# Projections that take turns in four PSUM banks, recurrence sums in the transposes' banks, and a difference issued behind a weight split

## The chip, the core and the metric

The kernel runs on one core of one Trainium2 chip. The metric is the device time of one execution in microseconds (us); the time before is a median of three executions. The profile comes from one further execution of the same program.

## What is computed

The kernel is a trunk of two layers over x with 1024 positions and 1024 channels, all in float32. Cut to what matters here, a layer is:

```
def hybrid_layer(x, ...):
    h = rms_norm(x, norm1_g)
    proj = h @ w_in                       # 4 mLSTM heads of 128, 8 attention heads of 64
    qk = silu(conv(concat([mq, mk])))     # centred depthwise conv, width 5
    h_fwd = mlstm_chunkwise(q, k, v, gi[0], gf[0])
    h_bwd = flip(mlstm_chunkwise(flip(q), flip(k), flip(v), ...))
    y_m = head_norm(h_fwd + h_bwd) * sigmoid(mo)
    y_a = dilated_attention(aq, ak, av)
    x = x + concat([y_m, y_a]) @ w_out
    u = relu(rms_norm(x, norm2_g) @ w_up)
    return x + (u * u) @ w_down
# inside mlstm_chunkwise, over the chunks of a direction:
    C_new = decay * C + einsum("bhs,bhsk,bhsv->bhkv", w, k_c, v_c)
    h = (s @ v + inter * (q @ C_prev)) / max(abs(den), exp(-m_t))
```

## The kernel before

Each float32 product of the projections and of the feed-forward is computed from parts. A weight tile of 128x512 is loaded, ScalarE casts it to the rounded part `wh` (line 80), GpSimd subtracts that from the weight to give the rest `wl` (line 82), and TensorE makes three matmuls for each slab of 128 channels: `wh` with the activations' high part (line 90), `wh` with their low part (line 91), and `wl` with the high part (line 92). In the output projection and the feed-forward the same three stand on line 835. A split's two instructions are given a high priority.

A projection of the mLSTM (`proj`, line 176) fills two banks of PSUM, one for each half of the 1024 positions. It loads the weights in two tiles of four slabs; for each tile it runs 12 matmuls into the bank of the first half and then 12 into that of the second. The banks come from a pool tagged `pj` with three buffers. VectorE empties a bank by multiplying with the norm's factors into SBUF (`evac_r`, line 174); such a tile is called z for q and k, so for the output gate and zv for the values.

For every head the order is: values (taken one head ahead), q, k, so (the output gate), then the values of the next head, and then the head's recurrence. After k's projection its conv (line 311) and SiLU (line 327) follow, and TensorE transposes k (line 361) and multiplies k with q (line 367) into tiles `pt` of the tag s, which has two buffers; ScalarE copies the transposes to `kn` (line 362) and VectorE multiplies the products into E (line 369). E also takes a transfer from the gates' table (E<-gd, line 344), a subtraction (line 345) and an exponential (line 347).

The recurrence runs over 8 chunks in two directions, one step of each direction in turn (14 steps that update the state). In a step TensorE adds two products into pn (line 383 with E, line 385 with the previous state C), and forms the new sum pk (line 394) in a bank of the tag t, which has one buffer; VectorE makes the new C out of it (line 399). The head before is closed (`m_tail`) around the start of the next recurrence; its multiplications and transposes stand on lines 414 to 431.

A scheduler decides the order of the instructions on each engine, from dependencies, the pools' buffers and priorities. The order in which the program is written and the priorities set it; `issue_after` holds instructions back until a given one has been placed.

The output projection and the feed-forward use a scheme with seven products of sums and differences of quarter matrices (`seven`, line 843; `products`, line 822, splits a weight tile and multiplies it). The first call in a layer (early) begins while the attention's last results are written: VectorE makes differences of y into T (lines 874, 793, 799), each of which is cast by ScalarE (line 783) and has its rest taken by VectorE (line 784), as operands b.

Of the kernel before, what the change touches and what calls it, by code (L numbers as in the profile page):

```python
# [12 lines left out]
F32 = mybir.dt.float32  # L13
# [6 lines left out]
P = 128  # L20
# [3 lines left out]
HALF = 512  # L24
# [8 lines left out]
NC = S // P  # L33
# [6 lines left out]
def bc(ap, shape):  # L40
    return ap.to_broadcast(shape)


class Trunk:
# [31 lines left out]
    def wsplit(self, raw):  # L76
        nc = self.nc
        with self.tc.high_priority(400):
            wh = self.wp.tile([P, 4, P], F32R, name="wh", tag="wh", bufs=3)
            nc.scalar.copy(wh, raw)  # L80
            wl = self.wp.tile([P, 4, P], F32R, name="wl", tag="wl", bufs=3)
            nc.gpsimd.tensor_tensor(out=wl, in0=raw, in1=wh.bitcast(F32), op=ALU.subtract)  # L82
        return wh, wl
# [7 lines left out]
        nc.tensor.matmul(ps, wh[:, j, :], xl[:, sl], start=False, stop=False)  # L91
        nc.tensor.matmul(ps, wl[:, j, :], xh[:, sl], start=False, stop=stop)  # L92

    def pj2(self):
        return [self.pj.tile([P, HALF], F32, name="pj", tag="pj", bufs=3) for _ in range(2)]


    def sumsq(self, acc, x, t, first, eng=None):
# [75 lines left out]
            self.nc.vector.tensor_tensor(out=out, in0=ps, in1=r[:, t * HALF:(t + 1) * HALF], op=ALU.mult)  # L174

    def proj(self, L, n, hs):
        ps = self.pj2()
        for i in range(2):
            w = self.wload(self.a["w_in"][L, n, :, 4 * i:4 * i + 4])
            for t in range(2):  # L180
                for j in range(4):
                    k = 4 * i + j
                    self.mm3(ps[t], w, j, hs[k], t, k == 0, k == KD - 1)
        return ps
# [4 lines left out]
    def gates(self, L, hs, acc, pl, order):  # L189

        nc = self.nc
        ps = [self.mx.tile([P, HALF], F32, name="ps", tag="s", bufs=2) for _ in range(2)]
# [4 lines left out]
                self.mm3(ps[t], ws[k // 4], k % 4, hs[k], t, k == order[0], k == order[-1])  # L197
        self.ws0 = None
        ws = [self.wload(self.a["w_in"][L, 4, :, 4 * i:4 * i + 4]) for i in range(2)]
        self.ahead = self.pj2()  # L200
        for t in range(2):
            for k in range(KD):
                if (t, k) == (1, (1, 0)[L]):
# [47 lines left out]
        for i in range(2):  # L251
            nc.vector.tensor_scalar(out=at[:, NC * i:NC * i + NC], in0=chunk, scalar1=v[:, i:i + 1], scalar2=None,
                                    op0=ALU.mult)
        pa = self.mx.tile([P, 2 * NC], F32, name="pa", tag="t", bufs=1)
        nc.tensor.matmul(pa, sel, at, start=True, stop=True)
        nc.vector.tensor_copy(st, pa)
        ML, BL = st[:, 0:NC], st[:, NC:2 * NC]
# [18 lines left out]
        pt = self.mx.tile([P, 3, NC, 16], F32, name="pt", tag="s", bufs=2)  # L276
# [6 lines left out]
    def m_values(self, L, h, hs, r, mp):  # L283
# [8 lines left out]
        return zv, v1  # L292

    def m_proj(self, L, h, hs, r, mp, gates, values):

        nc = self.nc
# [38 lines left out]
    def m_head(self, L, h, prj, nat, mp, pend):  # L335
        nc = self.nc
        q, k, so, v1 = prj
        G = lambda nm, shape: mp.tile(shape, F32, name=nm, tag="G", bufs=7)
        E, qi, dec = [], [], []
        for d in range(2):  # L340
            row = d * MH + h
            e = G("E", [P, NC, P])
            nc.sync.dma_start(e, bc(self.a["cm"][:, d:d + 1], [P, NC, P]))
            nc.gpsimd.dma_start(e, bc(self.gd[L][row, 0].unsqueeze(0), [P, NC, P]), accum_op=ALU.add)
            nc.vector.tensor_tensor(out=e, in0=nat[:, 0, :, row:row + 1].to_broadcast([P, NC, P]), in1=e,
                                    op=ALU.subtract)
            nc.scalar.activation(e, e, AF.Exp)
            E.append(e)
            x = G("qi", [P, S])
            nc.sync.dma_start(x.rearrange("p (c t) -> p c t", t=P), bc(self.gd[L][row, 1].unsqueeze(0), [P, NC, P]))  # L350
            dc = mp.tile([P, NC], F32, name="dec", tag="dec", bufs=4)
            nc.vector.tensor_copy(dc, x[:, (P - 1 if d == 0 else 0)::P])
            qi.append(x)
            dec.append(dc)
        for d in range(2):
            nc.vector.scalar_tensor_tensor(out=qi[d], in0=q, scalar=KSCALE, in1=qi[d], op0=ALU.mult, op1=ALU.mult)
        kn = G("kn", [P, NC, P])
        for g in range(2):
            pt = self.mx.tile([P, 4, P], F32, name="pt", tag="s", bufs=2)
            for c in range(4):  # L360
                nc.tensor.transpose(pt[:, c], k[:, (4 * g + c) * P:(4 * g + c + 1) * P], self.ident)
            nc.scalar.copy(kn[:, 4 * g:4 * g + 4], pt)
        for g in range(2):
            pt = self.mx.tile([P, 4, P], F32, name="pt", tag="s", bufs=2)
            for c in range(4):
                sl = slice((4 * g + c) * P, (4 * g + c + 1) * P)
                nc.tensor.matmul(pt[:, c], k[:, sl], q[:, sl], start=True, stop=True)
            for d in range(2):
                nc.vector.scalar_tensor_tensor(out=E[d][:, 4 * g:4 * g + 4], in0=pt, scalar=KSCALE,
                                               in1=E[d][:, 4 * g:4 * g + 4], op0=ALU.mult, op1=ALU.mult)  # L370
        if pend is not None:
            self.m_tail(*pend)
        H = [G("H", [P, NC, P + 2])[:, :, 0:P + 1] for d in range(2)]
        C = [None, None]
        pn = [None, None]
        for i in range(NC):
            for d in range(2):
                row = d * MH + h
                c = i if d == 0 else NC - 1 - i
                if i % 3 == 0:  # L380
                    pn[d] = self.mx.tile([P, 3, P + 1], F32, name="pn", tag="o", bufs=2)
                ps = pn[d][:, i % 3]
                nc.tensor.matmul(ps, E[d][:, c], v1[:, c], start=True, stop=i == 0)
                if i > 0:
                    nc.tensor.matmul(ps, qi[d][:, c * P:(c + 1) * P], C[d], start=False, stop=True)
                if i % 3 == 2 or i == NC - 1:
                    n = i % 3 + 1
                    dst = H[d][:, c - n + 1:c + 1] if d == 0 else H[d][:, c:c + n][:, ::-1]
                    nc.scalar.copy(dst, pn[d][:, :n])
                if i < NC - 1:  # L390
                    wv = mp.tile([P, P + 1], F32, name="wv", tag="wv", bufs=3)
                    nc.scalar.activation(wv, v1[:, c], AF.Copy, scale=nat[:, 1, c, row:row + 1])
                    pk = self.mx.tile([P, P + 1], F32, name="pk", tag="t", bufs=1)
                    nc.tensor.matmul(pk, kn[:, c], wv, start=True, stop=True)
                    Cn = mp.tile([P, P + 1], F32, name="C", tag=f"C{d}", bufs=2)
                    if i == 0:
                        nc.vector.tensor_copy(Cn, pk)
                    else:
                        nc.vector.scalar_tensor_tensor(out=Cn, in0=C[d], scalar=dec[d][:, c:c + 1],
                                                       in1=pk, op0=ALU.mult, op1=ALU.add)  # L400
                    C[d] = Cn
        return H
# [419 lines left out]
    def products(self, ws, parts, chain=False, ps=None, then=None):  # L822

        nc = self.nc
        new = ps is None
        res = []
        for q, w in enumerate(ws):
            out = self.bank(chain) if new else ps[q]
            wh, wl = self.wsplit(w)
            if then:  # L830
                then(q)
            for k in range(4):
                hi, lo = [x[:, k % 2] for x in parts[k // 2]]
                for i, (a, b) in enumerate(((wh, hi), (wh, lo), (wl, hi))):
                    nc.tensor.matmul(out, a[:, k, :], b, start=new and k + i == 0, stop=k + i == 5,  # L835
                                     skip_group_check=not new)
            res.append(out)
        return res
# [4 lines left out]
    def seven(self, src, B, op, take, nxt, early=False, end=None):  # L843
# [5 lines left out]
        T, T3 = [[self.up.tile([P, 2, HALF], F32, name="T", tag=tag, bufs=2) for _ in range(2)] for tag in ("T", "T3")]  # L849
# [12 lines left out]
        else:  # L862
# [4 lines left out]
            op = self.operand(B21)  # L867
# [3 lines left out]
        ps = self.products(w1, op)  # L871
# [3 lines left out]
        if not early:  # L875
            op = self.operand(T)
        take(2, ps)
        if not early:
            P5 = self.products(w2, op, then=addto(w2, 0, 0))
        op = self.negsum(T, B22)  # L880
        if not early:
            take(5, P5)
        chain = self.products(w2, op, True, chain, then=addto(w2, 0, 1))
        op = self.diff(T3, B22, B12)
        take(6, chain)
        chain = self.products(w0, op, True, chain)
        op = self.negsum(T, B21)
        take(7, chain)
        chain = self.products(w1, op, True, chain)
        op = self.operand(B22)  # L890
# [3 lines left out]
        ps = self.products(w2, op, ps=P5)  # L894
        op = nxt()
# [194 lines left out]
    def run(self):  # L1090
        tc, nc, a = self.tc, self.nc, self.a
        nc.scalar.preload_act_table_set("natural_log_exp_and_others")
        with tc.tile_pool(name="cst", bufs=1) as cp, tc.tile_pool(name="wp", bufs=1) as self.wp, \
                tc.tile_pool(name="hl", bufs=1) as self.hlp, tc.tile_pool(name="yx", bufs=1) as yxp, \
                tc.tile_pool(name="nrm", bufs=1) as self.nrm, tc.tile_pool(name="gnat", bufs=1) as self.gnat, \
                tc.tile_pool(name="pj", bufs=1, space=PSUM) as self.pj:
            self.L, self.pools = 0, ((yxp, "yx"), (self.hlp, "hl"))
            def const(nm, shape, eng=nc.sync):
                t = cp.tile(shape, F32, name=nm, tag=nm)
                eng.dma_start(t, a[nm])  # L1100
                return t
# [98 lines left out]
```

## Time and profile before

| | us |
|---|---|
| median of 3 executions | 2606.19 (2604.83 to 2611.5) |
| the profiled execution | 2613.41 |
| its span | 2611.6 |
| TensorE busy | 2456.4 |
| VectorE busy | 1906.1 |
| GpSimd busy | 1344.7 |
| ScalarE busy | 1244.6 |

The span is what the trace covers, from the first to the last instruction. Engines overlap, so busy times do not add up to it. A matmul of 128x512 is recorded with 0.39 us, but the matmuls overlap: one starts 0.23 us after the other at the full clock.

### The profile page before, as it was taken

Reading aid. Unit: us, or ns where it says so; the run is one execution under the profiler, and the core shown is the slowest. Engines: PE = TensorE matmul, PEld = TensorE weight load, DVE = VectorE, ACT = ScalarE, POOL = GpSimd, SP = SyncE. Lnnn points to the kernel's source line nnn. Section 1 sums busy time; section 2 is a strip of 40 time slices with the busy share of each in tenths; the row PEclk is TensorE's granted clock in tenths of the full one; section 3 lists DMA queues with packets and bytes.
Section 4 is the critical chain, followed back from the end, with each engine's and each line's share of the span. In section 5 each row is a group of like instructions: output and inputs, shape, how many; then the busy total and the mean of one; then the engine's idle time right before and its main releaser. Section 6 shows DMA issues by size and latency. Waiting matters only on the chain. (4 is left out here: it accounts for less than half of the span.)

```text
span 2611.6 us, 35935 instructions
## 1 busy us (share of the span) xinstructions
PE 2456.4 (94%) x13470; PEld 1952.3 (75%) x13470; DVE 1906.1 (73%) x2388; ACT 1244.6 (48%) x2068; POOL 1344.7 (51%) x1111
## 2 busy tenths in 40 slices
PE   7999989998999999999998999999899999999997
PEld 5778766666778888787776777666577787887876
DVE  6566776686886786968766666667768967679687
ACT  5444354454644545444543444445455445454554
POOL 4222332235676667767642223233276766667765
PEclk9999999998999999999999999999999999999998
DMA  4422100154555555555333221002455555545552
GB/s 144 119 81 81 43 25 22 40 140 105 102 108 115 105 108 104 111 106 115 96 112 98 81 81 39 21 24 80 109 117 98 108 108 114 106 108 104 110 102 80
DMA packets 136287, 239.65 MB, mean 92 GB/s; under 512 B 15008, under 2 KB 34480, under 8 KB 136112
## 3 DMA queue, kind: packets, MB, share of 16 engines
q0 software_dynamic: 49216, 101.45, 23.2%
q1 hardware_dynamic: 86896, 135.89, 17.0%
q8 instruction: 107, 1.75, 0.3%
q14 instruction: 68, 0.56, 0.1%
HBM read 228.50 MB, written 8.65 MB: 91 GB/s over the span
## 5 line engine op out<-in xcount | busy, mean ns | idle before, releaser
L82 POOL TENSOR_TENSOR wl<-w,wh 128x512 fp32r<-128x512 f32 x484 | 786.4, 1645 | 286.5 <-ACT wh L80 285.5
L835 PE MATMUL ph<-b,wh 128*128 128x512 f32 x2240 | 691.4, 390 | 0.2 <-ACT wh L80 0.2
L80 ACT CAST wh<-w 128x512 fp32r<-128x512 f32 x484 | 298.4, 618 | 415.2 <-PE ph L835 112.0
L835 PEld LDWEIGHTS ph<-b,wh 128*128 128x128 f32 x2240 | 421.1, 188 | 88.0 <-ACT wh L80 0.9
L835 PE MATMUL ph<-b,wl 128*128 128x512 f32 x1120 | 439.6, 393 | 9.7 <-POOL wl L82 9.2
L82 POOL TENSOR_TENSOR wl<-wr,wh 128x512 fp32r<-128x512 f32 x132 | 193.4, 1468 | 446.1 <-ACT wh L80 415.9
L835 PE MATMUL pj<-b,wh 128*128 128x512 f32 x1224 | 382.1, 394 | 22.9 <-ACT wh L80 14.9
L90 PE MATMUL pj<-hh,wh 128*128 128x512 f32 x896 | 369.2, 412 | 22.9 <-DVE z L174 21.8
L91 PE MATMUL pj<-hl,wh 128*128 128x512 f32 x896 | 357.4, 399 | 0.0
L92 PE MATMUL pj<-hh,wl 128*128 128x512 f32 x896 | 356.5, 398 | 0.7 <-POOL wl L82 0.7
L784 DVE TENSOR_TENSOR b<-T,b 128x1024 fp32r<-128x1024 f32 x144 | 249.0, 1733 | 120.4 <-ACT b L783 116.7
L835 PEld LDWEIGHTS pj<-b,wh 128*128 128x128 f32 x1224 | 231.9, 190 | 74.7 <-ACT wh L80 15.8
L835 PE MATMUL pj<-b,wl 128*128 128x512 f32 x612 | 241.2, 394 | 18.6 <-POOL wl L82 18.6
L835 PEld LDWEIGHTS ph<-b,wl 128*128 128x128 f32 x1120 | 210.6, 188 | 63.8 <-POOL wl L82 20.4
L90 PEld LDWEIGHTS pj<-hh,wh 128*128 128x128 f32 x896 | 171.1, 191 | 73.4 <-DVE z L174 24.4
L92 PEld LDWEIGHTS pj<-hh,wl 128*128 128x128 f32 x896 | 170.5, 190 | 36.5 <-POOL wl L82 1.6
L91 PEld LDWEIGHTS pj<-hl,wh 128*128 128x128 f32 x896 | 171.3, 191 | 30.8 <-issue 0.5
L783 ACT CAST b<-T 128x1024 fp32r<-128x1024 f32 x144 | 151.3, 1051 | 56.4 <-DVE T L799 20.5
L811 POOL DMA_DIRECT2D w<-w_down x128 | 117.3, 948 | 71.9 <-DMA w<-w_down 32.2
L617 ACT ACTIVATE sm<-sm,nm 128x512 f32<-128x512 f32 x128 | 91.6, 717 | 127.7 <-DVE nm L615 127.7
L835 PEld LDWEIGHTS pj<-b,wl 128*128 128x128 f32 x612 | 116.2, 190 | 47.1 <-POOL wl L82 22.8
L811 POOL DMA_DIRECT2D w<-w_up x128 | 115.0, 927 | 65.5 <-DMA w<-w_up 28.3
(256 smaller groups left out, 4159.9 us busy)
## 6 DMA issues: line engine op xcount, KB each, us to landing
w<-w_up SPq DMA_DIRECT2D x128, 256.0 KB, 2.7
w<-w_up POOLq DMA_DIRECT2D x128, 256.0 KB, 4.2
w<-w_down SPq DMA_DIRECT2D x128, 256.0 KB, 2.7
w<-w_down POOLq DMA_DIRECT2D x128, 256.0 KB, 4.3
wr<-w_in SPq DMA_DIRECT2D x116, 256.0 KB, 2.7
E<-cm SPq DMA_DIRECT2D x16, 512.0 KB, 5.8
qi<-gd SPq DMA_DIRECT2D x16, 512.0 KB, 7.0
E<-gd POOLq DMA_DIRECT2D x16, 512.0 KB, 7.2
```

The source lines that it names most:

```text
L80: nc.scalar.copy(wh, raw)
L82: nc.gpsimd.tensor_tensor(out=wl, in0=raw, in1=wh.bitcast(F32), op=ALU.subtract)
L90: nc.tensor.matmul(ps, wh[:, j, :], xh[:, sl], start=start, stop=False)
L91: nc.tensor.matmul(ps, wh[:, j, :], xl[:, sl], start=False, stop=False)
L92: nc.tensor.matmul(ps, wl[:, j, :], xh[:, sl], start=False, stop=stop)
L617: nc.scalar.activation(sm, sm, AF.Exp, scale=-1.0, bias=nm, accum_out=l)
L783: nc.scalar.copy(hi, src)
L784: nc.vector.tensor_tensor(out=lo, in0=src, in1=hi.bitcast(F32), op=ALU.subtract)
L811: self.nc.gpsimd.dma_start(w, src, accum_op=ALU.add)
L835: nc.tensor.matmul(out, a[:, k, :], b, start=new and k + i == 0, stop=k + i == 5, skip_group_check=not new)
```

## The change

Four edits are made. Every second projection of the mLSTM takes the bank of a new tile `pm` for its first half, with the tag t (one buffer), so four banks are used in turn: values pj and pj, q pm and pj, k pj and pj, so pm and pj. The sums `pk` and the gates' `pa` leave the tag t and take the tag s with its two buffers, which the transposes use. The copy of the transposed k to `kn` gets the high priority that weight splits have. In the early call of `seven`, the difference for the third product (`negsum`) is held back until the split of the third weight tile of the first product has been placed.

```diff
 def wsplit(self, raw):
-            nc.scalar.copy(wh, raw)
+            self.split = nc.scalar.copy(wh, raw).ins
...
-    def pj2(self):
-        return [self.pj.tile([P, HALF], F32, name="pj", tag="pj", bufs=3) for _ in range(2)]
+    def pj2(self, four=False):
+
+        res = []
+        for _ in range(2):
+            self.turn = (self.turn + 1) % 4
+            if four and self.turn == 3:
+                res.append(self.mx.tile([P, HALF], F32, name="pm", tag="t", bufs=1))
+            else:
+                res.append(self.pj.tile([P, HALF], F32, name="pj", tag="pj", bufs=3))
+        return res
...
     def proj(self, L, n, hs):
-        ps = self.pj2()
+        ps = self.pj2(True)
...
-        self.ahead = self.pj2()
+        self.ahead = self.pj2(True)
...
-        pa = self.mx.tile([P, 2 * NC], F32, name="pa", tag="t", bufs=1)
+        pa = self.mx.tile([P, 2 * NC], F32, name="pa", tag="s", bufs=2)
...
-            nc.scalar.copy(kn[:, 4 * g:4 * g + 4], pt)
+            with self.tc.high_priority(400):
+                nc.scalar.copy(kn[:, 4 * g:4 * g + 4], pt)
...
-                    pk = self.mx.tile([P, P + 1], F32, name="pk", tag="t", bufs=1)
+                    pk = self.mx.tile([P, P + 1], F32, name="pk", tag="s", bufs=2)
...
             wh, wl = self.wsplit(w)
+            if q == 2:
+                self.third = self.split
...
-        op = self.negsum(T, B22)
+        with self.tc.issue_after(self.third) if early else nullcontext():
+            op = self.negsum(T, B22)
```

What this does to the order of the instructions is shown at three places. Lines of the changed kernel stand 8 to 13 lower. The number of matmuls is the same.

On TensorE, this is the middle of head 0's recurrence in layer 0 before; the matmuls of lines 90 to 92 belong to the next projection (pj).

```order
L385 MATMUL pn<-C,qi 128x129
L383 MATMUL pn<-v_381,E 128x129
L91 MATMUL pj<-hl,wh 128x512
L394 MATMUL pk<-wv,kn 128x129
L385 MATMUL pn<-C,qi 128x129
L92 MATMUL pj<-hh,wl 128x512
L90 MATMUL pj<-hh,wh 128x512
L394 MATMUL pk<-wv,kn 128x129
```

And this is the same place in the changed kernel, from the recurrence's first state on (L392, L394 and L403 are the lines 383, 385 and 394 of before).

```order
L90 MATMUL pm<-hh,wh 128x512
L392 MATMUL pn<-v_381,E 128x129
L403 MATMUL pk<-wv,kn 128x129
L394 MATMUL pn<-C,qi 128x129
L403 MATMUL pk<-wv,kn 128x129
L392 MATMUL pn<-v_381,E 128x129
```

The projection's matmuls that stood between the steps, about one to a step, now stand behind the recurrence; within it three kinds follow each other without a break.

On ScalarE, this is the start of the output projection in layer 0 before: w_5587 to w_5589 are the first three weight tiles of the first product, b the parts of the operands.

```order
L783 CAST b<-y 128x1024
L783 CAST b<-T 128x1024
L80 CAST wh<-w_5587 128x512
L80 CAST wh<-w_5588 128x512
L80 CAST wh<-w_5589 128x512
L783 CAST b<-T 128x1024
```

And in the changed kernel:

```order
L792 CAST b<-y 128x1024
L80 CAST wh<-w_5587 128x512
L80 CAST wh<-w_5588 128x512
L80 CAST wh<-w_5589 128x512
L792 CAST b<-T 128x1024 x2
L80 CAST wh<-w_5590 128x512
```

The cast of the difference T that stood ahead of the first weight split now stands behind the third.

On VectorE, this is the row of work at the same place before; T are the differences and x the sums into which the first product goes.

```order
L874 TENSOR_TENSOR T<-y 128x1024
L784 TENSOR_TENSOR b<-y,b 128x1024
L874 TENSOR_TENSOR T<-y 128x1024
L799 SCALAR_TENSOR_TENSOR T<-y,T 128x1024 x2
L793 TENSOR_TENSOR T<-y 128x1024
L784 TENSOR_TENSOR b<-T,b 128x1024
L793 TENSOR_TENSOR T<-y 128x1024
L784 TENSOR_TENSOR b<-T,b 128x1024
L799 SCALAR_TENSOR_TENSOR T<-y,T 128x1024
L841 TENSOR_TENSOR x_4828<-x_4828,pj 128x512
```

And in the changed kernel (L885, L793, L808, L802 and L852 are the lines 874, 784, 799, 793 and 841 of before):

```order
L885 TENSOR_TENSOR T<-y 128x1024
L793 TENSOR_TENSOR b<-y,b 128x1024
L885 TENSOR_TENSOR T<-y 128x1024
L808 SCALAR_TENSOR_TENSOR T<-y,T 128x1024 x2
L802 TENSOR_TENSOR T<-y 128x1024 x2
L793 TENSOR_TENSOR b<-T,b 128x1024 x2
L852 TENSOR_TENSOR x_4828<-x_4828,pj 128x512
L808 SCALAR_TENSOR_TENSOR T<-y,T 128x1024 x2
```

Both differences of line 802 stand ahead of the parts b, and the second negated sum (line 808) has moved behind the first addition into x, so nine instead of ten operations stand ahead of that addition.

## Rows read from the trace of the kernel before

**Rows 1.** The page: busy us (share of the span) xinstructions
```profile
PE 2456.4 (94%) x13470; PEld 1952.3 (75%) x13470; DVE 1906.1 (73%) x2388; ACT 1244.6 (48%) x2068; POOL 1344.7 (51%) x1111
```

**Rows 2.** TensorE's waits: waited for, us in total, times, longest
```profile
PE pj L90 <- DVE z L174: 21.8, 6, 4.0
PE pj L835 <- POOL wl L82: 18.6, 8, 5.1
PE pj L835 <- ACT wh L80: 14.9, 2, 7.4
...
PE pt L367 <- ACT kn L362: 13.3, 3, 8.1
```

**Rows 3.** Timeline of PE: start, duration, in brackets idle time and what ended it
```profile
138.88 0.80 PE L90 MATMUL pj<-hh,wh 128*128 128x512 f32 x1 [3.87 <-DVE z L174]
...
266.54 0.50 PE L90 MATMUL pj<-hh,wh 128*128 128x512 f32 x1 [3.71 <-DVE z L174]
...
1555.67 0.50 PE L90 MATMUL pj<-hh,wh 128*128 128x512 f32 x1 [3.62 <-DVE z L174]
```

**Rows 4.** Timeline of DVE in layer 0, head 1
```profile
126.58 0.68 DVE L174 TENSOR_TENSOR z<-pj,r 128x512 f32<-128x512 f32 x1
...
138.14 1.28 DVE L174 TENSOR_TENSOR z<-pj,r 128x512 f32<-128x512 f32 x2
```

**Rows 5.** Windows behind three stalls; PEclk is the granted clock
```profile
138.90:144.10 5.20, 5.20 (x12) 4.11 (x13) 3.91 (x4) 1.23 (x2) 0.00 (x0) 0.50 0.00 0
1427.60:1431.00 3.40, 3.40 (x9) 2.61 (x8) 2.79 (x3) 0.96 (x2) 0.00 (x0) 0.50 0.00 0
1492.40:1495.80 3.40, 3.40 (x10) 2.66 (x9) 2.88 (x3) 1.07 (x3) 0.00 (x0) 0.50 0.00 0
```

**Rows 6.** Timelines in layer 0, heads 1 and 3: ACT, then PE
```profile
145.95 1.06 ACT L327 ACTIVATE c<-c 128x1024 f32<-128x1024 f32 x1
...
275.45 1.04 ACT L329 ACTIVATE c<-c 128x1024 f32<-128x1024 f32 x1
...
160.51 1.03 PE L361 MATMUL pt<-ident,c 128*128 128x128 f32 x8
...
276.45 0.93 PE L361 MATMUL pt<-ident,c 128*128 128x128 f32 x7
```

**Rows 7.** Timeline of PE in head 0's recurrence, layer 0
```profile
103.17 0.46 PE L394 MATMUL pk<-wv,kn 128*128 128x129 f32 x2
...
103.61 0.47 PE L92 MATMUL pj<-hh,wl 128*128 128x512 f32 x1
...
104.17 0.46 PE L394 MATMUL pk<-wv,kn 128*128 128x129 f32 x2
```

**Rows 8.** Timeline of DVE in the same recurrence
```profile
103.67 0.35 DVE L399 SCALAR_TENSOR_TENSOR C<-C,dec,pk 128x129 f32<-128x129 f32 x1 [0.64 <-PE pk L394]
```

**Rows 9.** Timeline of ACT at the output projection, layer 0
```profile
596.87 1.05 ACT L783 CAST b<-y 128x1024 fp32r<-128x1024 f32 x1 [7.85 <-DVE y L679]
...
602.92 1.66 ACT L80 CAST wh<-w 128x512 fp32r<-128x512 f32 x3
```

**Rows 10.** Timeline of PE at the output projection, layer 0
```profile
603.59 1.22 PE L835 MATMUL pj<-b,wh 128*128 128x512 f32 x2 [7.43 <-ACT wh L80]
609.87 0.79 PE L835 MATMUL pj<-b,wl 128*128 128x512 f32 x1 [5.06 <-POOL wl L82]
```

**Rows 11.** Timelines of POOL, then DVE, at the output projection, layer 0
```profile
603.62 6.20 POOL L82 TENSOR_TENSOR wl<-w,wh 128x512 fp32r<-128x512 f32 x1 [13.65 <-ACT wh L80]
...
597.26 1.22 DVE L874 TENSOR_TENSOR T<-y 128x1024 f32<-128x1024 f32 x1
...
607.48 1.22 DVE L799 SCALAR_TENSOR_TENSOR T<-y,T 128x1024 f32<-128x1024 f32 x1
```

**Rows 12.** Timelines of POOL, then DVE, later in layer 0
```profile
674.96 1.95 POOL L82 TENSOR_TENSOR wl<-w,wh 128x512 fp32r<-128x512 f32 x1
...
675.68 2.31 DVE L784 TENSOR_TENSOR b<-B,b 128x1024 fp32r<-128x1024 f32 x1
```

More of the change, by code (lines that the diff above doesn't have):

```diff
@@ L1096, in run @@
                 tc.tile_pool(name="pj", bufs=1, space=PSUM) as self.pj:
+            self.turn = 0
             self.L, self.pools = 0, ((yxp, "yx"), (self.hlp, "hl"))
```

## The prediction

> **What bounds the kernel now.** I read the page first. TensorE is busy for 94% of the span [rows 1], so the time is its matmuls plus the gaps between them, and an edit that leaves the matmuls as they are can only act on gaps, on the rate at which matmuls are issued, and on the granted clock. So I read TensorE's waits next [rows 2] and looked up each wait that the diff touches in the timelines. Six waits of a projection for the emptying of a bank make 21.8 us. At the output projections there are 14.9 us for the first weight's cast and, within the 18.6 us of the row above it, two waits for the first rest wl. In the first heads 13.3 us go to the copy kn. The reader is to see that these 60-odd us are spread over a dozen places, each with its own last releaser, and that each place has to be read by itself.
>
> The six are all of one kind. In heads 1 to 3 of either layer the output gate's projection (so) has made 12 matmuls into the bank of its first half, and the first matmul into the other half waits 2.9 to 4.0 us until VectorE has emptied k's first half [rows 3]. There are three banks, and VectorE comes to k's evacuation late: at 138.14, behind the conv of q and the closing of the head before [rows 4]. The matmul starts at 138.88. Behind a stall the granted clock is 0.50 for a while, which is the lower of the two levels, 1.2 GHz [rows 5].
>
> **The fourth bank, heads 1 and 2.** With four banks so's first half takes the bank of q's first half, and its second half that of q's second half. The second of q's evacuations is the row at 126.58, over at 127.3 [rows 4]; so's second half comes up at 138.88 - 3.87 = 135.0 [rows 3]. That leaves 7.7 us, and the two evacuations of k, which stay where they are on VectorE, are then needed only by the next head's values, 24 + 24 matmuls of 0.23 us later. So the stall goes. What could be late next is k's transpose: it starts at 160.51, its input's SiLU ends at 147.0 [rows 6]. Brought forward by the stall and its slow stretch, 6.5 us, it would start at 154.0, still 7 us behind its input, since the next head's values projection (48 matmuls, 10.9 us) lies between. In heads 1 and 2 the whole stall is therefore a gain: 21.8 less head 3's 3.71 and 3.62 [rows 2, 3] is 14.5 us in four stalls. The half clock gives back half of its length: 5.2 us in the first, and 3.4 us in each of layer 1's [rows 5], so 2.6 + 1.7 + 1.7 = 6.0 us; the fourth stall shows none, and I count nothing for it. Together 20.5 us; if the clock falls all the same, 14.5.
>
> **Head 3.** The last head has no values projection between so and the transposes. In layer 0 the SiLU of q ends at 276.49 and the transposes start at 276.45 [rows 6], directly behind so. If so came 3.7 + 1.7 us earlier, the transposes would wait for the SiLU and the products' operands, a chain on VectorE and ScalarE that the fourth bank doesn't shorten. What shortens it is the recurrence of the head before: its 14 steps hold about 14 projection matmuls of 0.23 us, 3.2 us in all, which now stand behind it, so the closing work on VectorE starts some 3 us earlier against the projections. I take 3 us in each layer, 6 in all; bounds nothing and the full 3.71 + 3.62 + 1.7 = 9.0 us.
>
> **The recurrence.** A step is bound by the one bank of pk: pk starts at 103.17 and 104.17 [rows 7]; VectorE starts on it at 103.67 and is done at 104.02 [rows 8]; the next pk may only then write. The matmuls in a step take about 0.9 us (two projection matmuls of 0.23 and four small ones of some 0.11), so 0.1 us a step is hidden loss, at most 8 recurrences x 14 steps x 0.1 = 11 us. In the new order the projection matmuls leave, a step's matmuls then need 6 x 0.11 = 0.67 us, and the second bank lets pk of one direction run beside the C of the other. A product with C stands five small slots (1.1 us) and more behind its pk; the chain needs 0.85 us up to the end of C. It fits, with little over, and the copies of H at the changes of the pn tiles can hold it up. No row shows a step without filling; I take 2 us of gain of the 11, near nothing because the latency stays close to what it has to fit in. The loss is bounded under the rivals. The sharing of the tag s with pt and the move of pa I cost at nothing: the transposes' tiles are emptied before the recurrence's second step, and pa occurs once a layer.
>
> **kn.** The copy has a higher priority, but in the new order it stands in head 0 behind the same two instructions of ScalarE as before, an exponential of E that waits for a transfer, and a weight's cast. The 13.3 us [rows 2] stay: 0.
>
> **The output projection.** Before, the first cast of a weight waits on ScalarE behind the cast of a difference; three casts start at 602.92 [rows 9], and TensorE starts at 603.59 after 7.43 us [rows 10]. Now they follow the cast of y, some 5 us earlier, at about 598. But after two matmuls TensorE needs the rest wl. Before, GpSimd's wl began at 603.62 and took 6.20 us, and TensorE waited 5.06 us more for it [rows 10, 11]. VectorE ran without a gap through ten operations with two inputs from SBUF, from 597.26 to 608.70 [rows 11]; wl ended at 609.82, 1.1 us behind the last of them. I read this as GpSimd kept out until the row of operations broke off. The changed order has nine of them ahead of the first addition, so the row ends 1.14 us earlier, and TensorE gets its wl 1.1 us earlier although wh is there 5 us earlier. That is 1.1 us in each layer, 2.2 in all. The other end is that wl gets in at the first boundary between two of VectorE's operations, as later in the same layer, where it took 1.95 us and it was VectorE's next operation that was longer, 2.31 us [rows 12]. Then wl would be there by 598.5 + 2 = 600.6 instead of 609.8: 9 us a layer, 18 in all. I take the first, because the place, the engines and the kinds of operation are the same as in the row that shows it.
>
> The Trainium skill speaks for the other end: "SBUF — State Buffer", section "SBUF: two separate sides", has an exclusive lock between VectorE with two SBUF inputs and GpSimd, held for a whole instruction by whichever starts first. By that rule the blocked engine waits for one instruction, as at 674.96, and the sum would have 18 us here; the 6.20 us at 603.62 disagree with it.
>
> **The sum.** 20.5 + 6 + 2 + 2.2 = 30.7 us. The profiled execution took 2613.4 us, 7.2 us more than the median; off that it gives 2582.7, and off the median, 2606.2, about 2575.5. I name 2575.5.
>
> **Rivals.** GpSimd gets in at the output projection: 16 us more, 2559.5. For it, the many wl that wait for one operation only; against it, the one row at this very place.
>
> kn moves all the same, by what else comes earlier: 13.3 us more, 2562. Against it, the order.
>
> The stalls only move: the E chain, which waits for its own transfers, holds heads 1 and 2 to the 3 us that the recurrence frees, 4 x 3 = 12, head 3 and the recurrence give nothing, and with 2.2 the gain is 14: 2592. Against it stand the 7 us to spare in front of the transposes.
>
> The edits do nothing that lasts: the scheduler's gains are used up by waits elsewhere, about 2606.
>
> The recurrence becomes a chain of latencies, and the kernel slower. Filling has gone out of it, so whatever a step takes beyond 0.67 us is lost. If a step stays at the 1.00 us of [rows 7], 8 x 14 x 0.33 = 37 us are lost, which eats the gain of the others (28.7) and ends at 2614.5. It decides for slower from a step of 1.00 us on: 28.7 + 7.8 us over 112 steps is 0.33. For it, that the chain of pk and C alone took all of a step before; against it, the second bank, which breaks that chain.
>
> **Chances.** The likeliest 0.50; GpSimd in early 0.25; kn too 0.04; moved stalls 0.09; no effect 0.07; slower 0.05. The measurement tells 0.3%, 7.8 us, from no change. Faster is 0.88, the same 0.07, slower 0.05. The range takes the bounds: at the upper end 14.5 us alone, 2591.7, which holds the moved stalls nearly; at the lower end 20.5 + 9 + 7 of the recurrence's 11 + 18 = 54.5, 2551.7. So 2552 to 2592.
>
> **What would show it.** Right: no wait of line 90's successor for z; k's transposes of heads 1 and 2 start some 6 us earlier against the preceding projection; in head 3 a new wait of the transposes or of their products of 1 to 3 us; pk every 0.67 to 0.75 us; kn's waits as before; at the output projection two matmuls at 598.5, counted on the old time axis, and a wait of 8 to 10 us for wl. Wrong: wl of 2 us there; pk every 0.9 us or more with TensorE idle or at the granted clock of 0.50 in the recurrence; a wait of so for a cast of wh behind an exponential.

## The result and the profile after

| | before | changed |
|---|---|---|
| median, us | 2607.53 (2604.83 to 2611.5) | 2580.63 (2573.73 to 2581.38) |
| ratio, 95% interval | | 0.989 (0.9868 to 0.9912) |
| the profiled execution, us | 2613.41 | 2581.37 |

The change takes 26.9 us off the median; the interval of the ratio is 23 to 34 us. The forecast was 30.7 us and 2575.5, with a range that holds the result. The sum was near; most of its terms were not. What follows is mostly about that.

The page of the changed kernel, its span and its first row, beside [rows 1]:

```profile
span 2579.6 us, 35988 instructions
...
PE 2451.5 (95%) x13470; PEld 1954.0 (76%) x13470; DVE 1897.8 (74%) x2388; ACT 1241.0 (48%) x2068; POOL 1342.9 (52%) x1111
```

TensorE's busy time fell by 4.9 us only, so most of the time came out of its gaps. Its waits in the changed kernel, beside [rows 2]:

```profile
PE ph L846 <- POOL wl L82: 14.5, 19, 2.7
PE pt L376 <- ACT kn L371: 14.2, 2, 10.1
...
PE pj L846 <- POOL wl L82: 11.1, 8, 1.6
PE pt L369 <- ACT c L335: 8.0, 2, 4.0
...
PE pj L846 <- ACT wh L80: 4.7, 2, 2.3
```

The same first row in the kernel before:

```profile
PE ph L835 <- POOL wl L82: 9.2, 12, 1.4
```

The row for z is gone: no projection of a head waits for VectorE to empty a bank. kn's waits stay, as forecast. Three rows are to be looked at. The wait of the transposes (line 369) for k's SiLU, 4.0 us in either layer, is new and is that of head 3. Both waits at the start of the output projection have become small, not only the one for wh. And the products that go into ph, of the output projection and of the feed-forward, wait 5.3 us more for wl than before.

**Recurrence.** TensorE in head 1's recurrence of layer 0:

```profile
162.61 0.39 PE L403 MATMUL pk<-wv,kn 128*128 128x129 f32 x2
162.84 0.39 PE L392 MATMUL pn<-v,E 128*128 128x129 f32 x2
...
163.28 0.39 PE L403 MATMUL pk<-wv,kn 128*128 128x129 f32 x2
```

A step is 0.67 us, just what its six matmuls need at 0.11 us each, where it was 1.00 us for four of them and two larger ones [rows 7]. Nothing is lost in it any more.

**Head 3.** VectorE in layer 0, with the subtraction of E (line 353), q's conv (line 319) and k's evacuation (line 182):

```profile
239.69 1.23 DVE L353 TENSOR_TENSOR E<-nat,E 128x1024 f32<-128x1024 f32 x1 [3.53 <-DMA E<-gd]
...
242.71 2.33 DVE L353 TENSOR_TENSOR E<-nat,E 128x1024 f32<-128x1024 f32 x1 [1.05 <-DMA E<-gd]
244.96 2.59 DVE L319 SCALAR_TENSOR_TENSOR c<-z,cw,c 128x1024 f32<-128x1024 f32 x2
...
253.60 1.28 DVE L182 TENSOR_TENSOR z<-pj,r 128x512 f32<-128x512 f32 x2
```

And TensorE behind it:

```profile
263.41 0.77 PE L369 MATMUL pt<-ident,c 128*128 128x128 f32 x5 [4.00 <-ACT c L335]
```

VectorE stands idle for 3.53 and 1.05 us at the two transfers of E, in front of q's conv, although the conv doesn't need E. k's evacuation, its conv and its SiLU queue behind that.

**Output projection.** GpSimd at the first split in layer 0:

```profile
585.21 2.21 POOL L82 TENSOR_TENSOR wl<-w,wh 128x512 fp32r<-128x512 f32 x1 [9.77 <-ACT wh L80]
```

VectorE around it:

```profile
583.95 1.22 DVE L885 TENSOR_TENSOR T<-y 128x1024 f32<-128x1024 f32 x1
585.08 1.22 DVE L793 TENSOR_TENSOR b<-y,b 128x1024 fp32r<-128x1024 f32 x1
586.22 2.29 DVE L885 TENSOR_TENSOR T<-y 128x1024 f32<-128x1024 f32 x1
588.43 4.52 DVE L808 SCALAR_TENSOR_TENSOR T<-y,T 128x1024 f32<-128x1024 f32 x2
...
598.83 0.67 DVE L852 TENSOR_TENSOR x<-x,pj 128x512 f32<-128x512 f32 x1
```

And TensorE, from the first product (pj) to the second (ph):

```profile
585.18 1.22 PE L846 MATMUL pj<-b,wh 128*128 128x512 f32 x2 [2.33 <-ACT wh L80]
587.48 0.80 PE L846 MATMUL pj<-b,wl 128*128 128x512 f32 x1 [1.08 <-POOL wl L82]
...
601.34 0.73 PE L846 MATMUL ph<-b,wh 128*128 128x512 f32 x2 [1.16 <-ACT wh L80]
602.96 0.50 PE L846 MATMUL ph<-b,wl 128*128 128x512 f32 x1 [0.89 <-POOL wl L82]
...
609.89 0.50 PE L846 MATMUL ph<-b,wl 128*128 128x512 f32 x1 [1.18 <-POOL wl L82]
```

The first wl takes 2.21 us, not the 6.20 of [rows 11]; it ends 1.1 us behind the first boundary of VectorE's row (585.08 + 1.22 = 586.30), so it got in there, and the next operation of VectorE is the longer for it (2.29 us). Where TensorE waited 7.43 + 5.06 us [rows 10], it now waits 2.33 + 1.08, a gain of 9.1. But the nine operations of VectorE ahead of the first addition now take 598.83 - 583.95 = 14.9 us, where at 1.14 us apiece they would take 10.3. ScalarE's next weight cast is queued behind that addition, and the second product waits three times, 3.2 us, where before none of these waits was there.

### The profile page after: what moved, and what is told of

The parts are those of the page before. It is cut to its first block, busy times and chain, and to the rows that moved or that the text cites. A ratio compares the mean times of both kernels' runs of the same rounds, so it can differ in the third digit from the quotient of the medians.

```text
span 2579.6 us, 35988 instructions
## 1 busy us (share of the span) xinstructions
PE 2451.5 (95%) x13470; PEld 1954.0 (76%) x13470; DVE 1897.8 (74%) x2388; ACT 1241.0 (48%) x2068; POOL 1342.9 (52%) x1111
## 5 line engine op out<-in xcount | busy, mean ns | idle before, releaser
L82 POOL TENSOR_TENSOR wl<-w,wh 128x512 fp32r<-128x512 f32 x484 | 774.0, 1619 | 287.7 <-ACT wh L80 286.7
L846 PEld LDWEIGHTS ph<-b,wh 128*128 128x128 f32 x2240 | 421.6, 188 | 90.9 <-ACT wh L80 3.9
L846 PE MATMUL ph<-b,wl 128*128 128x512 f32 x1120 | 440.9, 394 | 14.9 <-POOL wl L82 14.5
L793 DVE TENSOR_TENSOR b<-T,b 128x1024 fp32r<-128x1024 f32 x144 | 248.4, 1729 | 122.6 <-ACT b L792 119.0
L90 PE MATMUL pj<-hh,wh 128*128 128x512 f32 x768 | 312.9, 407 | 0.6 <-ACT wh L80 0.6
L92 PE MATMUL pj<-hh,wl 128*128 128x512 f32 x768 | 301.7, 393 | 0.2 <-POOL wl L82 0.2
L91 PE MATMUL pj<-hl,wh 128*128 128x512 f32 x768 | 301.5, 393 | 0.0
L90 PEld LDWEIGHTS pj<-hh,wh 128*128 128x128 f32 x768 | 145.2, 189 | 44.3 <-issue 16.8
L92 PEld LDWEIGHTS pj<-hh,wl 128*128 128x128 f32 x768 | 145.0, 189 | 32.2 <-POOL wl L82 1.3
L91 PEld LDWEIGHTS pj<-hl,wh 128*128 128x128 f32 x768 | 145.1, 189 | 27.1 <-issue 0.5
```

The lines of the kernel that those rows point to most:

```text
L90: nc.tensor.matmul(ps, wh[:, j, :], xh[:, sl], start=start, stop=False)
L793: nc.vector.tensor_tensor(out=lo, in0=src, in1=hi.bitcast(F32), op=ALU.subtract)
```

## The experiments

The runs were timed in other series than the changed kernel (2580.63), each beside the kernel before. The 95% interval of each ratio reaches 3 to 7 us to either side, so a difference of a few us between two of these kernels is not told from none by the times alone.

### Without the fourth bank

```diff
-            if four and self.turn == 3:
+            if False:
```

> The changed kernel with three banks for all projections, all else as in it. Theory: the fourth bank carries 20.5 us (four stalls of heads 1 and 2, 14.5, and 6.0 of slow clock behind them), head 3 nothing: about 2601, six waits of so for z of 21 to 23 us, and the 4.0 us waits of head 3's transposes gone. Rival: the closed-up recurrence carries most of the gain; then it stays below 2592.

Measured 2589.38 us, ratio to before 0.9923 (0.9909 to 0.9938). Its waits for z:

```profile
PE pj L90 <- DVE z L182: 16.6, 8, 3.0
```

The rival's bound (2592) was right and the theory's number 12 us off: the fourth bank is worth 8.8 us here by the medians (some 2 to 15 by the intervals). The six waits come back as eight, and shorter than [rows 2], 16.6 instead of 21.8 us, so something else in the change had shortened them. Two of the eight are head 3's, 5.6 us; its new wait, 8.0 us, is gone. So in head 3 the bank buys one wait for a longer one, and its gain is in heads 1 and 2.

### The move of the recurrence's sums alone

```diff
-        pa = self.mx.tile([P, 2 * NC], F32, name="pa", tag="t", bufs=1)
+        pa = self.mx.tile([P, 2 * NC], F32, name="pa", tag="s", bufs=2)
...
-                    pk = self.mx.tile([P, P + 1], F32, name="pk", tag="t", bufs=1)
+                    pk = self.mx.tile([P, P + 1], F32, name="pk", tag="s", bufs=2)
```

> The kernel before with only pk and pa moved to the transposes' tag. Theory: the recurrences lose their hidden 7 us, steps of pk become 0.67 us: about 2601, the six waits for z stay. Rival: the projection matmuls that left the recurrence are missing there and steps stay near 0.9 us: 2607 or more.

Measured 2597.6 us, 10.9 less than before in the same comparison (2608.49), ratio 0.9951 (0.9932 to 0.997). Its waits:

```profile
PE pj L835 <- ACT wh L80: 14.9, 2, 7.4
...
PE pj L90 <- DVE z L174: 14.1, 8, 3.0
```

By the medians this is the largest of the parts. The theory had expected some 7 us of it, and the six waits for z to stay; they fall from 21.8 to 14.1 us with no bank added. Some 14 projection matmuls (3.2 us) left each recurrence and now stand behind it, so the recurrence is over that much earlier against the projections, and with it the work that VectorE has to do in front of k's evacuation. The waits for z are 7.7 of the 10.9 us.

### The hold: taken away, and alone

```diff
-        with self.tc.issue_after(self.third) if early else nullcontext():
+        with nullcontext():
             op = self.negsum(T, B22)
```

> The changed kernel without the hold of the difference. Theory: the hold is worth what stands in the trace after the second product, 3.9 + 2.9 = 6.8 us: about 2587.5, with the wait for wh back at 7 us and that for wl at 5 us in either layer. Rival (the prediction's term): 2.2 us, 2583.

Measured 2583.1 us, ratio 0.9896 (0.988 to 0.9913), 2.5 us above the changed kernel; the intervals overlap, so the times decide neither for the theory's 6.8 nor for the rival's 2.2. TensorE's two waits at the first product (7.4 and 5.1 us) and the duration of GpSimd's first wl, to the hundredth, are those of before:

```profile
PE pj L846 <- POOL wl L82: 19.9, 9, 5.1
PE pj L846 <- ACT wh L80: 14.9, 2, 7.4
```

```profile
592.20 6.20 POOL L82 TENSOR_TENSOR wl<-w,wh 128x512 fp32r<-128x512 f32 x1 [14.03 <-ACT wh L80]
```

The traces tell more than the times. Here are the first matmul of the output projection of layer 0 and the first one behind it (line 137, line 129 before). The first two rows are of this run, the third is of the changed kernel, the last of the kernel before:

```profile
592.17 1.22 PE L846 MATMUL pj<-b,wh 128*128 128x512 f32 x2 [7.43 <-ACT wh L80]
678.46 1.02 PE L137 MATMUL pj<-acc,ones 128*128 128x512 f32 x2
...
673.70 1.02 PE L137 MATMUL pj<-acc,ones 128*128 128x512 f32 x2
...
690.36 1.02 PE L129 MATMUL pj<-acc,ones 128*128 128x512 f32 x2
```

From the end of the attention's last matmul to there it is 678.46 - (592.17 - 7.43) = 93.7 us in this run, 673.70 - (585.18 - 2.33) = 90.9 in the changed kernel and 690.36 - (603.59 - 7.43) = 94.2 before. In layer 1 the three are 94.7, 91.3 and 94.0. The stretch scatters by some 1 us between traces of kernels in which it has the same instructions: the five that have this hold and none of the later ones there show 90.9 to 91.9 us in layer 0 and 91.3 to 92.9 in layer 1 (means 91.5 and 92.2), the three without any hold 92.9 to 94.2 and 94.0 to 94.8 (means 93.6 and 94.5). So the hold keeps about 2.1 and 2.3 us, 4.4 in all, between theory and rival: of the 9 us that it wins at the first product about a quarter is left at the end of the projection.

The second run puts the hold, with the two lines that record the third split, into the kernel before:

```diff
-        op = self.negsum(T, B22)
+        with self.tc.issue_after(self.third) if early else nullcontext():
+            op = self.negsum(T, B22)
```

> The kernel before with only the hold. Theory: the output projection is its own place, so the gain is again about 7 us, 2600.5, and the first wl takes about 2.2 us instead of 6.2, since it meets VectorE's row at another point. Rival: the first wl again stays out for the whole row of VectorE, takes 10 us, and the gain is 2 us, 2605.

Measured 2604.72 us against 2608.49, ratio 0.9986 (0.9976 to 0.9997). Its first wl:

```profile
603.32 2.22 POOL L82 TENSOR_TENSOR wl<-w,wh 128x512 fp32r<-128x512 f32 x1 [9.83 <-ACT wh L80]
```

So the theory's mechanism (a wl of 2.2 us) was right, and the gain, 3.8 us with an interval of 1 to 6, is nearer to the rival's 2 than to the theory's 7. Alone, the hold removes 9 us of waits in a layer and keeps about 2.

### Is the first wl kept out by VectorE?

The kernel before, with the difference for the third product held behind the first addition. ScalarE's order is as before.

```diff
-        op = self.diff(T3, B22, B12)
+        with self.tc.issue_after(self.added[first]) if early else nullcontext():
+            op = self.diff(T3, B22, B12)
```

> The kernel before with only the difference for the third product held behind the first addition, so that ScalarE's order at the split is as before, but VectorE's row behind the first wl is two operations shorter and has a gap in it. Theory (kept out by VectorE): the first wl ends at that gap or at the end of the row, after 2 to 5 us instead of 6.20. Rival (a fixed delay of the first wl behind a long idle time of GpSimd): 6.20 us again. The time: 1 to 4 us a layer less than before by the first, no gain at that wait by the second.

Measured 2604.9 us against 2609.2, ratio 0.9988 (0.9977 to 0.9999), 0 to 6 us less. GpSimd, then VectorE, then TensorE:

```profile
606.79 1.79 POOL L82 TENSOR_TENSOR wl<-w,wh 128x512 fp32r<-128x512 f32 x1 [13.99 <-ACT wh L80]
```

```profile
606.22 1.23 DVE L784 TENSOR_TENSOR b<-T,b 128x1024 fp32r<-128x1024 f32 x1
607.48 2.18 DVE L799 SCALAR_TENSOR_TENSOR T<-y,T 128x1024 f32<-128x1024 f32 x1
609.59 2.30 DVE L784 TENSOR_TENSOR b<-T,b 128x1024 fp32r<-128x1024 f32 x1
```

```profile
606.76 1.22 PE L835 MATMUL pj<-b,wh 128*128 128x512 f32 x2 [7.43 <-ACT wh L80]
608.64 0.80 PE L835 MATMUL pj<-b,wl 128*128 128x512 f32 x1 [0.66 <-POOL wl L82]
```

The idle time of GpSimd ahead of it is the same 14 us, and wl takes 1.79 us, so a fixed delay after a long pause is out. Where VectorE's operations left a small gap (0.03 us between 607.45 and 607.48), GpSimd got in, and from there on the two take turns. That GpSimd was kept out by VectorE's row is what this shows. Why that row kept it out and the one at 674.96 [rows 12], also without a gap, did not, stays open. The kinds of operation and the point at which wl comes do not settle it. In the changed kernel a later wl met the same pair, T and then b, also without a gap and at nearly the same point (some 0.6 us into T, against 0.7 at 603.62), and got in at the first boundary:

```profile
594.64 2.04 POOL L82 TENSOR_TENSOR wl<-w,wh 128x512 fp32r<-128x512 f32 x1
```

GpSimd had been issuing transfers just before that one, and had been idle for 13.65 us ahead of the one at 603.62 [rows 11]. Whether a long pause lets it lose its turn where there is no gap was not tested.

### q's conv ahead of E

```diff
+            if i == 0:
+                self.conv = conv.ins
...
-            nc.vector.tensor_tensor(out=e, in0=nat[:, 0, :, row:row + 1].to_broadcast([P, NC, P]), in1=e,
-                                    op=ALU.subtract)
+            with self.tc.issue_after(self.conv) if h > 0 else nullcontext():
+                nc.vector.tensor_tensor(out=e, in0=nat[:, 0, :, row:row + 1].to_broadcast([P, NC, P]), in1=e,
+                                        op=ALU.subtract)
```

> The changed kernel with the two subtractions of E of heads 1 to 3 held behind q's conv on VectorE. Theory: in head 3 the transposes wait 4.0 us for k's SiLU because VectorE stands in order at the transfers E<-gd ahead of q's conv; with the conv first the wait falls below 2 us in either layer and the time by 4 to 7 us to about 2575. Rival: the chain is bound by the projections' own ends and by the closing of the head before; then the waits stay at 4 us and the time at 2580.

Measured 2567.48 us, ratio to before 0.9848 (0.983 to 0.9866): 13 us below the changed kernel (4 to 18 by the intervals), more than expected; the two traced executions differ by 7.8. VectorE in head 3 of layer 0:

```profile
239.70 0.68 DVE L182 TENSOR_TENSOR z<-pj,r 128x512 f32<-128x512 f32 x1
241.60 6.15 DVE L319 SCALAR_TENSOR_TENSOR c<-z,cw,c 128x1024 f32<-128x1024 f32 x4 [1.22 <-ACT c L317]
247.67 2.35 DVE L356 TENSOR_TENSOR E<-nat,E 128x1024 f32<-128x1024 f32 x2
249.94 1.28 DVE L182 TENSOR_TENSOR z<-pj,r 128x512 f32<-128x512 f32 x2
```

The two subtractions no longer wait for their transfers, the conv starts at 241.60 instead of 244.96, k's evacuation at 249.94 instead of 253.60, and the transposes' 4.0 us are gone: what is left at head 3 is 0.6 us at each of three places. E was late enough to be done last and stood first.

The expectation names the waits alone. Behind them the changed kernel also ran at half the clock, for 3.4 us in layer 0 and 6.8 in layer 1 (the number before the last two is the granted clock):

```profile
264.10:267.50 3.40, 3.27 (x15) 2.76 (x14) 3.17 (x3) 3.37 (x6) 1.81 (x1) 0.50 0.02 5
1533.80:1540.60 6.80, 6.06 (x27) 5.91 (x28) 5.04 (x7) 6.63 (x8) 1.80 (x1) 0.50 0.13 41
```

With q's conv first the granted clock is 1.00 at both places, which gives back about half of 10.2 us.

### kn ahead of the exponentials, in head 0

```diff
+        if h == 0:
+            for e in E:
+                with self.tc.issue_after(copied.ins):
+                    nc.scalar.activation(e, e, AF.Exp)
```

> The changed kernel with the exponentials of E of head 0 held behind the copies kn on ScalarE. Theory: the 14.2 us before kn come from the exponential that stands ahead and waits for a transfer; then most of them go, and a shorter wait for E at the first product of the recurrence takes their place: 5 to 9 us less, about 2573. Rival: E is needed at once behind kn, so the wait only moves and the time stays within 2 us of 2580.

Measured 2573.06 us, ratio to before 0.9865 (0.9849 to 0.9881), 7.6 us below the changed kernel, though the intervals overlap. The wait that takes the place of kn's 14.2 us:

```profile
PE pn L397 <- DVE E L383: 8.6, 2, 7.4
```

As expected, part of the wait moves to E: 5.6 us of it are gone; the other 2.0 us are within the scatter of the runs. The priority that the change gives to the copy moved no instruction on any engine (the program is the same with and without it); naming what the copy must come before did.

### The third product's difference behind the first addition

The edit of the run on VectorE's row, now made to the changed kernel.

> The changed kernel with the difference for the third product held behind the first addition of the output projection. Theory: the addition is late because it stands behind nine operations of VectorE, which GpSimd lengthens; two operations less bring it 2.3 us earlier, the waits of the second product (1.2, 0.9, 1.2 us in layer 0) shrink, and the time falls by 2 to 4 us. Rival: the third product's parts come late instead, and the time stays at 2580 or rises.

Measured 2570.0 us, ratio to before 0.9854 (0.9839 to 0.9869), 10.6 us below the changed kernel (3 to 16 by the intervals). VectorE at the output projection of layer 0:

```profile
587.10 4.52 DVE L808 SCALAR_TENSOR_TENSOR T<-y,T 128x1024 f32<-128x1024 f32 x2
591.55 2.42 DVE L793 TENSOR_TENSOR b<-T,b 128x1024 fp32r<-128x1024 f32 x2
593.89 0.68 DVE L852 TENSOR_TENSOR x<-x,pj 128x512 f32<-128x512 f32 x1
```

TensorE's waits of the second product in it:

```profile
PE ph L846 <- POOL wl L82: 1.0, 2, 0.6
```

The addition comes 593.89 - 587.10 = 6.8 us after the start of the negated sums, where it came 598.83 - 588.43 = 10.4 us after it, and the second product's waits fall from 3.2 to 1.0 us. This is a part of what the hold had won and given back. At the end of the projection less of it is left:

```profile
583.85 0.73 PE L846 MATMUL pj<-b,wh 128*128 128x512 f32 x2 [2.33 <-ACT wh L80]
...
670.76 1.02 PE L137 MATMUL pj<-acc,ones 128*128 128x512 f32 x2
```

From the attention's last matmul on it is 670.76 - (583.85 - 2.33) = 89.2 us, and 90.3 in layer 1, where the mean with the first hold alone was 91.5 and 92.2. So 4.2 of the 10.6 us stand at the place of the edit, near the expected 2 to 4. Most of the rest is not the edit's. In the feed-forward of layer 0 the traced execution of the changed kernel has one wait that is longer than in any other trace, with a granted clock of 0.50 for 6.8 us behind it:

```profile
889.33 0.79 PE L846 MATMUL ph<-b,wl 128*128 128x512 f32 x1 [2.73 <-POOL wl L82]
```

In this run, and in the two before it, that wait is 0.5 to 1.0 us and the clock behind it 1.00, though none of the three edits touches the place; some 3 to 4 us of each of the three traced differences lie there. Whether the other executions of the changed kernel have that wait too is not known.

### All three, and what the parts of the change are worth then

The last three edits together:

> The three holds together. Theory: three different places, so the gains add: 11 to 20 us below the changed kernel, 2560 to 2570. Rival: each gain is passed on to the next wait, and less than 6 us is left.

Measured 2555.38 us, ratio to before 0.9794 (0.9779 to 0.9809): 25 us below the changed kernel, a little more than expected, though less than the three one by one (31), each of which may hold the same few us of scatter. The same with three banks:

> The version with the three holds, with three banks for all projections. Theory: the waits of so are a matter of how late VectorE comes to k's evacuation; with q's conv ahead of E it comes some 3 us earlier, so that most of the six waits are gone without a fourth bank: 2556 to 2560. Rival: the fourth bank is worth the same 9 us as in the changed kernel, 2564.

Measured 2555.05 us, ratio 0.9796 (0.9771 to 0.9821). Its wait for z:

```profile
PE pj L90 <- DVE z L182: 1.8, 2, 1.3
```

With VectorE in time, the fourth bank is worth nothing that can be measured (the interval is some 8 us to either side). q's conv ahead of E with three banks and without the other two holds was not run. And without the hold of the negated sum:

> The version with the three holds, without the hold of the negated sum. Theory: with the other difference behind the first addition nothing is given back, so the hold is now worth its whole wait, about 5 us a layer for wh: 2562 to 2566. Rival: it is worth the 2.5 us that it was worth in the changed kernel, 2558.

Measured 2564.07 us, ratio 0.9844 (0.9817 to 0.9871): the hold, worth 2.5 us by the medians in the changed kernel and 4.4 by the traces, is worth 8.7 us by the medians once the addition behind it is early. The traces bear that out: the two output projections take 92.6 and 94.2 us without it, 88.9 and 89.5 in the mean of the three kernels with both holds, 8.4 us in all.

## Why the prediction was right

The number was right, and the steps were so in part. That the sum came within 4 us is in part luck: head 3 was given some 6 us too much and the output projection some 2 too little, and most of what the bank got too much the move of the sums got too little.

- **The fourth bank, heads 1 and 2** (20.5 us). The mechanism was right: no wait for z is left in the trace. Its size as a term of its own was not: 8.8 us when the bank is taken away. Either the bank or the recurrence's shift takes off part of the same waits, and I gave the whole to the bank and counted the shift again in head 3. Together with the recurrence and head 3 the terms were 28.5 us; the kernel without the hold shows 2608.49 - 2583.1 = 25.4 (23 to 31).
- **Head 3** (6 us). This step failed. "What shortens it is the recurrence of the head before": the closing work did come earlier, but VectorE then stood at the transfers of E, which come in order ahead of q's conv. The wait of 3.71 us for a bank became one of 4.00 for the SiLU, with a slow clock behind it, so the gain was nothing. The rival "the stalls only move" had the cause, the E chain, and had put it to heads 1 and 2, where the values projection covers it.
- **The recurrence** (2 of at most 11 us). Steps run at 0.67 us with no loss. The edit alone gives 10.9 us, but 7.7 of them are shorter waits for z; the 3 that are left are near the 2. What I missed is that the same edit shortens the waits that I had put to the bank. The chain of pk and C that I was careful about holds no step up any more with the second bank; the rival of a slower kernel had nothing to it.
- **kn** (0). Right: 13.3 us before, 14.2 after.
- **The output projection** (2.2 us). The size was near (2.5 us by the medians of the changed kernel with and without the hold, 4.4 by the traces) and the mechanism wrong, so the size was luck. I took GpSimd to be kept out again. It got in, as the rival said; the waits fell by 9 us in a layer, not by 1.1, and about three quarters of that were given back in the products behind, since each turn that GpSimd takes lengthens VectorE's row. I had looked at the wait removed and not at what stands behind the row on VectorE, the first addition, and on ScalarE behind that, the next cast.

The Trainium skill, "SBUF — State Buffer", section "SBUF: two separate sides", has VectorE with two SBUF inputs and GpSimd exclude each other for a whole instruction. By that rule the one that comes in delays the other by an instruction, and the trace after agrees: 2.21 us for wl, 2.29 for VectorE's next. The 6.20 us of the runs without either hold, five operations of VectorE long, go beyond it.

## What to carry to other kernels

When a matmul waits for a bank, ask first why the engine that empties it is late: here it stood, in order, at a transfer that its next work didn't need, and with that wait put behind (and two more holds in place) a further bank was superfluous. Two edits that shorten the same wait don't add; price them together, or one after the other. And when a wait in front of one product goes, follow the engines that were busy meanwhile to the next thing that they release, because a gain can be given back in the products behind, and a second, small move there can win part of it again.

## What was not expected of the hardware

GpSimd's subtraction of 128x512 took 6.20 us in every run in which it met the long row of VectorE at the same point, in both layers (before, before with the sums moved, and the changed kernel without the hold), and about 2.2 us, 1.8 in the two kernels with the third product's difference held but not the negated sum, where the row was met elsewhere or had a gap of 0.03 us. In the second case VectorE pays: operations of 1.2 us were recorded with 2.2 to 2.3 us.
